# Eight gate chunks by Strassen's scheme, all gates by way of DRAM, a written order for the branches, and the residual made during the attention

## The chip, the cores and the metric

The kernel runs on one core of a Trainium2 chip. Its time is the device time in microseconds of one launch, given as the median of several runs. The engines are TensorE (PE: matmuls; PEld: its weight loads), VectorE (DVE), ScalarE (ACT), GpSimd (POOL) and SyncE (SP, which here only issues DMAs). Each engine works through its own queue in program order and waits at the head of the queue for what other engines or DMAs have still to deliver.

## The reference

One encoder block on 1024 tokens of width 1024. The stage that matters here lies between the attention and the feed-forward part:

```python
proj = h @ w_in[l] + b_in[l]
qa, ka, va, qb, kb, vb, ga, gb = jnp.split(proj, IN_SPLITS, axis=-1)
...
y_na = neighbourhood_attention(qa, ka, va, na_rpb[l]) @ w_branch_na[l]
y_swa = windowed_gqa_with_sink(qb, kb, vb, swa_sink[l]) @ w_branch_swa[l]
mixed = jax.nn.sigmoid(ga) * y_na + jax.nn.sigmoid(gb) * y_swa
attn_out = mixed @ w_out[l] + b_out[l]
h = layer_norm(DEEPNORM_ALPHA * h + attn_out, ln1_g[l], ln1_b[l])
```

The two gates `ga` and `gb` are products of the 1024 x 1024 normalised input with 1024 columns of weights each. The residual `DEEPNORM_ALPHA * h + b_out` does not depend on the attention.

## The kernel before

**Three products for one.** Every float32 product is made from high and low parts: `hi*hi + hi*lo + lo*hi` (`gemm3`, lines 219 to 226). An operand is split by a copy on ACT (the high part) and a subtraction on DVE (the low part). A chunk of 128 gate columns takes 2 token halves x 8 pieces of depth x 3 = 48 matmuls of 128x512. `hT` (64 KB of each partition) holds the normalised input, both parts, transposed.

**The attention** (lines 603 to 703) is written out by hand in steps of two query blocks (`steps`, line 668): normalise (`part_a2`), scores (`part_a`), transposes (`part_b`), products with the values (`part_c`). Between them `pump` lets PE do matmuls of the projections, so that it has work while DVE and ACT make the softmax; these "fills" include the gate chunks f = 4 to 7 of both gates (`N_AHEAD = 4`), whose sums go to DRAM (`sg_d`). Sixteen heads of four steps; heads 8 to 15 get 72 fills each, heads 0 to 7 get 48. The fills are used up when the last three steps (62 to 64) come. At each head from 7 on POOL makes the bias of a later head (`na_bias`), from 16 small loads on SP's queue.

**Gates and branches** (lines 704 to 796) are not in a written order: a planner places their instructions, also among the attention's last ones. `oS` holds the attention's output, split (lines 714 to 721). For each f from 0 to 7: for f < 4 two gate chunks are made from `hT` and go through the sigmoid straight from PSUM (lines 770 to 780); for f >= 4 the stored sums are read back from DRAM. Then two branch products per token half (`w_na`, `w_swa`) are multiplied by the gates on DVE and added on POOL into `mx` (lines 785 to 792). In the same stage POOL makes the residual, two operations for each of eight token groups, from DRAM to DRAM (`residual0`, lines 756 to 761), and `wo`, the output projection's weights, is loaded and split (lines 799 to 804).

**Later** the feed-forward products already use the Winograd form of Strassen's scheme; its list of seven products with the PSUM bank of each is

```python
STEPS = ((1, "a"), (2, "b"), (6, "a"), (5, "c"), (7, "a"), (3, "c"), (4, "a"))
```

The functions that the diff touches follow with their line numbers.

Of the kernel before, what the change touches and what calls it, by code (L numbers as in the profile page):

```python
# [75 lines left out]
def encoder_block(ctx, tc, x, w_in, w_na, w_swa, w_out, w_ff1, w_ff2, par, rows, rpbp, sink,  # L76
# [4 lines left out]
    def b32(ap):  # L81
        return ap.bitcast(F32)
# [26 lines left out]
    sg_d = dp.tile([N_AHEAD, 2, 2, P, 512], F32, name="sg_d")  # L109
    e_d = dp.tile([8, 8, 31, 24], F32, name="e_d")  # L110


# [31 lines left out]
    def load_w(srcs):  # L144
        return split_w(dma_w(srcs))
# [7 lines left out]

    hT = r1p.tile([P, 2, NK, S], F32R, tag="r1", name="hT")
    ln = r3p.tile([P, 8, D], F32, tag="r3", name="ln")
    actx = ExitStack()
    ap = actx.enter_context(tc.tile_pool(name="ap", bufs=2, reuse_waits="tile"))

# [236 lines left out]
    def gate_half(i, w, half):  # L395

        f, gi = 8 - N_AHEAD + i // 2, i % 2
        ps = psum("mm")
        yield from gemm3_steps(ps, w, lambda part, k: h_perm(part, k, half))

        def evac():
            s_ = wp.tile([P, 512], F32, tag="wlo2" if i == 1 else "whi2", name="sa", bufs=1)
            ACT.activation(s_, ps, AF.Identity, bias=prm[:, C_G + gi * 8 + f:C_G + gi * 8 + f + 1], scale=1.0)
            nc.sync.dma_start(sg_d[i // 2, gi, half], s_)
        defer(0, evac)

    def gate_ahead(i):
# [132 lines left out]
    def part_c(s):  # L540
# [62 lines left out]
    with tc.manual_schedule(engines=MANUAL):  # L603
# [19 lines left out]
        def pump(n):  # L623
            for _ in range(n):
                if next(fill, "end") == "end":
                    for e in later:
                        e[0] = 0
                    flush()
                    return
                for e in later:  # L630
                    e[0] -= 1
# [33 lines left out]
            pass  # L665
        next(fill)

        def steps(s, n):
# [7 lines left out]
            pump(part[0])  # L676
            if 0 <= s < 64:
# [4 lines left out]
            pump(part[1])  # L682
            if s >= 1:
# [10 lines left out]
        oT = r3p.tile([P, 8, S], F32, tag="r3", name="oT")  # L694
        counts = [CNT[0]] * 8 + [CNT[1]] * 8
        for H in range(16):
            if H >= 7 and H - 7 < 8:
# [3 lines left out]
        for s in range(62, 65):  # L701
            steps(s, TAIL)
        pump(1000)
    actx.close()
    n_w[:] = [0, 3]


    xp = ctx.enter_context(tc.tile_pool(name="xp", bufs=1, side="right", reuse_waits="tile"))
    r2x = ExitStack()
    r2p = r2x.enter_context(tc.tile_pool(name="r2p", bufs=1, side="right", reuse_waits="tile"))  # L710
    oS = r2p.tile([P, 2, 8, S], F32R, tag="r2", name="oS")
    mctx = ExitStack()
    mp = mctx.enter_context(tc.tile_pool(name="mp", bufs=2, reuse_waits="tile"))
    for c in range(8):
        src, hi, lo = oT[:, c, :], oS[:, 0, c, :], oS[:, 1, c, :]
        if c >= 4:

            src = src.rearrange("p (r g c) -> p g r c", g=NCG, c=8)
            hi, lo = (t.rearrange("p (g r c) -> p g r c", g=NCG, c=8) for t in (hi, lo))
        ACT.copy(hi, src)  # L720
        DVE.tensor_tensor(out=lo, in0=src, in1=b32(hi), op=ALU.subtract)
    mx = r3p.tile([P, 8, S], F32, tag="r3", name="mx")

    def o_na(part, k, half):
        return oS[:, part, k, half * 512:(half + 1) * 512]

    def o_swa(part, k, half):
        return oS[:, part, 4 + k, half * 512:(half + 1) * 512]

    def tok(g):  # L730
        return slice(g * P, (g + 1) * P)

    mhl = {}

    def split_mx(g):

        m = xp.tile([P, 2, 8, P], F32R, tag=f"m{g % 2}", name="m")
        mhl[g] = m[:, 0], m[:, 1]
        ACT.copy(m[:, 0], mx[:, :, tok(g)])
        DVE.tensor_tensor(out=m[:, 1], in0=mx[:, :, tok(g)], in1=b32(m[:, 0]), op=ALU.subtract)  # L740

    def branch_w(f):
        fs = slice(f * P, (f + 1) * P)
        return load_w([(0, 4, 0, P, w_na[:, fs]), (4, 4, 0, P, w_swa[:, fs])])


    r01 = xp.tile([P, 2, D], F32, tag="m0", name="r01")
    zr = xp.tile([P, 2, D], F32, tag="m1", name="zr")
    for i in range(2):
        nc.sync.dma_start(r01[:, i, :], row_bc(i))  # L750
    nc.sync.dma_start(zr[:, 0, :], row_bc(2))
    for i in range(2):
        POOL.tensor_scalar(out=r01[:, i, :], in0=r01[:, i, :], scalar1=ALPHA, scalar2=None, op0=ALU.mult)
    POOL.tensor_tensor(out=r01[:, 1, :], in0=r01[:, 1, :], in1=zr[:, 0, :], op=ALU.add)

    def residual0(g):
        z = zr[:, g % 2, :]
        nc.sync.dma_start(z, xn0_d[g])
        POOL.tensor_tensor(out=z, in0=z, in1=r01[:, 0, :], op=ALU.mult)
        POOL.tensor_tensor(out=z, in0=z, in1=r01[:, 1, :], op=ALU.add)  # L760
        nc.sync.dma_start(xr0_d[g], z)

    wbs = {}
    for f in range(8):
        if f < 4:
            residual0(2 * f)
            residual0(2 * f + 1)
        sg = []
        for gi in range(2):
            w = load_w(gate_w(gi, f)) if f < 8 - N_AHEAD else None  # L770
            for half in range(2):
                s_ = mp.tile([P, 512], F32, tag=f"sg{gi}", name="sg")
                sg.append(s_)
                if w is None:
                    nc.sync.dma_start(s_, sg_d[f - 8 + N_AHEAD, gi, half])
                    ACT.activation(s_, s_, AF.Sigmoid)
                    continue
# [3 lines left out]
        for i in (f, f + 1):  # L781
            if i not in wbs and (i == f or 8 - N_AHEAD <= i < 8):
                wbs[i] = branch_w(i)
        wb = wbs[f]
        for half in range(2):
            pa = psum("t")
            gemm3(pa, wb, lambda part, k: o_na(part, k, half), nk=4)
            DVE.tensor_tensor(out=sg[half], in0=pa, in1=sg[half], op=ALU.mult)
            pb = psum("o")
            gemm3(pb, wb, lambda part, k: o_swa(part, k, half), nk=4, k0=4)  # L790
            DVE.tensor_tensor(out=sg[2 + half], in0=pb, in1=sg[2 + half], op=ALU.mult)
            POOL.tensor_tensor(out=mx[:, f, half * 512:(half + 1) * 512], in0=sg[half], in1=sg[2 + half], op=ALU.add)
            if f == 7 and half == 0:
                split_mx(0)
                split_mx(1)
    mctx.close()


    wo = r1p.tile([P, 2, NK, D], F32R, tag="r1", name="wo")
    for k in range(NK):  # L800
        raw = wp.tile([P, D], F32, tag="raw", name="raw", bufs=2)
        nc.sync.dma_start(raw, w_out[k * P:(k + 1) * P, :])
        ACT.copy(wo[:, 0, k, :], raw)
        DVE.tensor_tensor(out=wo[:, 1, k, :], in0=raw, in1=b32(wo[:, 0, k, :]), op=ALU.subtract)
# [143 lines left out]
    with tc.manual_schedule(engines=MANUAL):  # L948
# [28 lines left out]
                raws[2] = head_w(2)  # L977

        def more_ring(i):
            t = xp.tile([P, 2, 2, 512], F32R, tag=f"m{i}", name="twx")  # L980
            ring[0:0] = [t[:, 0], t[:, 1]]

        us, snaps = {}, {}
# [337 lines left out]
        for n, (p, i) in enumerate(seq):  # L1321
# [5 lines left out]
            elif n == 2:  # L1327
                more_tw()
            if n == 12:
                xts.append(xp.tile([P, 2, D], F32, tag="m1", name="rr"))  # L1330
                xts.append(xp.tile([P, 4, 512], F32, tag="m0", name="rst"))
                residual_rows()
            ff1_mm(p, i)
            for f in tails[:2 if p == 1 else 1]:
# [273 lines left out]
```

## Time and profile before

| | us |
|---|---|
| median of 3 runs (1376.11 to 1378.56) | 1377.28 |
| the profiled execution: its time | 1378.37 |
| the profiled execution: its span, first to last instruction | 1376.6 |
| PE busy | 1336.7 |
| DVE busy | 934.1 |
| ACT busy | 679.6 |
| POOL busy | 295.5 |

The granted clock was 0.992 of full on average. A row of the profile is read like this: line of the kernel, engine, operation, output<-inputs, shapes, xcount, then busy time and mean duration, then the idle time of the engine before these instructions and what ended it. In a timeline the first number is the start in us from the first instruction, the second the time that the row's instructions took, and what stands in brackets is idle time before, with who ended it. A table of stages gives for each engine its busy time in the stretch and the number of instructions.

### The profile page before, as it was taken

The page shows a single profiled execution, that of the slowest core. Times are in us where ns is not written, and L with a number is a line of the kernel's source. Part 1 is how long each engine was busy: PE and PEld are TensorE (multiplying, and loading weights), DVE is VectorE, ACT ScalarE, POOL GpSimd, SP SyncE. Part 2 cuts the span into 40 slices and gives each one's busy share as a digit, 9 for nine tenths or more (in the row PEclk, how much of TensorE's full clock was granted, in tenths as well). Part 3 has the DMA queues.
Part 4 walks back from the last instruction along what each step waited for, and adds up shares of the span by engine and source line. Part 5 has one row for each costly group of instructions (what it writes and reads, how often), then busy time and mean ns, then how long its engine had stood idle before and what let it go on. Part 6 is the DMA issues. An engine that isn't in the chain of part 4 may idle for free. (4 is left out here: it accounts for less than half of the span.)

```text
span 1376.6 us, 17188 instructions
## 1 busy us (share of the span) xinstructions
PE 1336.7 (97%) x6312; PEld 1102.1 (80%) x6312; DVE 934.1 (68%) x1553; ACT 679.6 (49%) x1173; POOL 295.5 (21%) x264
## 2 busy tenths in 40 slices
PE   5999999999999999999999999999999999999996
PEld 4788888888888888888888788888887888878884
DVE  7458989877776721244467987676655668787777
ACT  4436666666655611142445755555554533333354
POOL 3332212121120375011000042222100001121218
PEclk9999999999999999999999999999999999999998
DMA  6521021112102444144233576655528554544323
GB/s 217 181 66 43 24 62 44 32 34 51 38 22 77 127 164 156 59 155 151 89 110 130 164 242 205 207 195 181 197 94 319 191 184 145 206 145 179 116 96 123
DMA packets 130165, 179.70 MB, mean 131 GB/s; under 512 B 26400, under 2 KB 82976, under 8 KB 126368
## 3 DMA queue, kind: packets, MB, share of 16 engines
q1 hardware_dynamic: 129648, 178.48, 39.1%
q8 instruction: 49, 0.80, 0.3%
q14 instruction: 36, 0.29, 0.1%
q10 hardware_dynamic: 432, 0.12, 0.0%
HBM read 124.04 MB, written 54.72 MB: 130 GB/s over the span
## 5 line engine op out<-in xcount | busy, mean ns | idle before, releaser
L234 PE MATMUL ps_mm<-hT,whi 128*128 128x512 f32 x832 | 275.8, 406 | 7.2 <-DVE hT L210 2.5
L234 PEld LDWEIGHTS ps_mm<-hT,whi 128*128 128x128 f32 x832 | 154.8, 191 | 38.4 <-DVE kl L298 4.3
L234 PE MATMUL ps_mm<-hT,wlo 128*128 128x512 f32 x416 | 170.7, 410 | 0.0
L494 ACT ACTIVATE ss<-ss,st 128x384 f32<-128x384 f32 (+1 forms) x128 | 74.5, 586 | 64.7 <-DVE st L482 35.0
L1228 ACT CAST t<-stg 128x2048 fp32r<-128x2048 f32 x28 | 53.5, 1909 | 88.6 <-PE ps_o L1360 47.3
L1379 POOL TENSOR_TENSOR acc<-acc,rst 128x512 f32<-128x512 f32 x16 | 30.7, 1917 | 302.4 <-DMA rst<-xr_d 289.5
L1360 PE MATMUL ps_mm<-t,t 128*128 128x512 f32 x384 | 93.0, 397 | 2.3 <-DVE t L1231 1.6
L1360 PE MATMUL ps_s<-t,t 128*128 128x512 f32 x384 | 91.0, 392 | 0.0
L1360 PEld LDWEIGHTS ps_mm<-t,t 128*128 128x128 f32 x384 | 72.9, 191 | 20.0 <-DVE t L1231 2.5
L234 PEld LDWEIGHTS ps_mm<-hT,wlo 128*128 128x128 f32 x416 | 79.3, 191 | 11.5
L1360 PEld LDWEIGHTS ps_s<-t,t 128*128 128x128 f32 x384 | 72.1, 188 | 16.2
L945 PE MATMUL ps_t<-hS,tw 128*128 128x512 f32 x348 | 84.8, 392 | 0.0
L534 ACT CAST pth<-ps_t 128x384 fp32r<-128x384 f32 (+1 forms) x128 | 52.0, 456 | 64.2 <-PE ps_t L531 63.7
L1231 DVE TENSOR_TENSOR t<-stg,t 128x2048 fp32r<-128x2048 f32 x28 | 68.1, 2431 | 14.8 <-ACT t L1228 14.8
L945 PEld LDWEIGHTS ps_t<-hS,tw 128*128 128x128 f32 x348 | 65.4, 188 | 14.8
L150 DVE TENSOR_TENSOR wlo<-raw,whi 128x1024 fp32r<-128x1024 f32 x16 | 24.9, 1558 | 76.1 <-ACT whi L149 76.0
L1360 PE MATMUL ps_t<-t,t 128*128 128x512 f32 x288 | 68.6, 392 | 0.3 <-DVE t L1231 0.3
L1360 PE MATMUL ps_o<-t,t 128*128 128x512 f32 x288 | 68.0, 392 | 0.0
L537 DVE TENSOR_TENSOR ptl<-ps_t,pth 128x384 fp32r<-128x384 f32 (+1 forms) x128 | 61.2, 518 | 7.2 <-ACT pth L534 6.8
L1360 PEld LDWEIGHTS ps_t<-t,t 128*128 128x128 f32 x288 | 54.0, 188 | 13.0 <-DVE t L1231 1.2
L1360 PEld LDWEIGHTS ps_o<-t,t 128*128 128x128 f32 x288 | 54.1, 188 | 11.9
L1112 DVE TENSOR_TENSOR usl<-usl 128x512 f32<-128x512 f32 x64 | 50.8, 794 | 14.8 <-ACT usl L1005 11.1
(258 smaller groups left out, 3139.6 us busy)
## 6 DMA issues: line engine op xcount, KB each, us to landing
us_d<-usl SPq DMA_DIRECT2D x112, 256.0 KB
stg<-us_d SPq DMA_DIRECT2D x28, 1024.0 KB
raw<-in_w_ff SPq DMA_DIRECT2D x36, 512.0 KB
raw<-in_w_in SPq DMA_DIRECT2D x26, 512.0 KB
w2b<-in_w_ff SPq DMA_DIRECT2D x7, 1024.0 KB
w2a<-in_w_ff SPq DMA_DIRECT2D x5, 1024.0 KB
sg_d<-sa SPq DMA_DIRECT2D x16, 256.0 KB
xn_d<-ln SPq DMA_DIRECT2D x8, 512.0 KB
```

The lines of the kernel that those rows point to most:

```text
L150: DVE.tensor_tensor(out=lo, in0=raw, in1=b32(hi), op=ALU.subtract)
L234: PE.matmul(ps, a[:, k, :], act(b, k), start=(k == 0 and i == 0), stop=(k == NK - 1 and i == 2))
L494: ACT.activation(p[:, :n], p[:, :n], AF.Exp, bias=st[:, 2 + i:3 + i], scale=0.125, accum_out=st[:, 4 + i:5 + i])
L534: ACT.copy(pth[:, a:b, :], pv)
L537: DVE.tensor_tensor(out=ptl[:, a:b, :], in0=pv, in1=b32(pth[:, a:b, :]), op=ALU.subtract)
L945: PE.matmul(ps, ww, act[:, part, k, :], start=(first and k == 0 and m == 0), stop=(k == 3 and m == 2), skip_group_check=True)
L1112: DVE.tensor_tensor(out=out, in0=a, in1=b, op=op)
L1228: ACT.copy(slot[:, :, 0, :], src)
L1231: DVE.tensor_tensor(out=slot[:, :, 1, :], in0=src, in1=b32(slot[:, :, 0, :]), op=ALU.subtract)
L1360: PE.matmul(ps, st[:, a, part, j * P:(j + 1) * P], w[:, a, wpart, :], start=(first and a == 0 and m == 0), stop=(a == 3 and m == 2), skip_ ...
L1379: POOL.tensor_tensor(out=z, in0=z, in1=t, op=ALU.add)
```

## The change

**The last eight gate chunks** (f = 0 to 3 of both gates) become four pairs p of 256 columns: p = 0 and 1 are chunks 0/1 and 2/3 of the first gate, p = 2 and 3 those of the second. With the input cut in depth (K1, K2) and tokens (T1, T2), A11 = hT[K1,T1], A12 = hT[K2,T1], A21 = hT[K1,T2], A22 = hT[K2,T2], and the weights of a pair cut in depth and columns (B11 to B22), seven products of 12 matmuls each (a block (p, i)) replace eight:

- i = 1: A11 B11, i = 2: A12 B21; C11 is their sum
- i = 6: S2 (B22 - (B12 - B11)), i = 5: S1 (B12 - B11), i = 7: S3 (B22 - B12), i = 3: S4 B22, i = 4: A22 (B21 - the sum of i = 6)
- S1 = A21 + A22, S2 = S1 - A11, S3 = A22 - S2, S4 = A12 - S2

PSUM bank a gathers products 1, 6, 7 and 4 in turn and is read out after each; the other banks are added on DVE. All finished gates go to DRAM (`sg_d` grows from 4 to 8 chunks), and the branches read every gate back and apply the sigmoid then.

**The order** of everything from the end of the attention to the last split of `wo` is written out for all engines. S1 is summed in the last head (`s1_sum`, one DVE operation of 128x2048 after each of three steps). The weights of blocks (0,1), (0,2), (1,1) and (1,2) are loaded and split in the last steps; blocks (0,1) and (0,2) run inside steps 63 and 64, the others after the attention. The last evacuation of the attention (`last_evac`) is put off behind the first sum for S2. `graw` holds a pair's raw columns: pairs 2 and 0 share one 8 KB buffer (`x0p`), pair 1 takes the one in which S1 was summed (`x1p`), pair 3 half of `gt`, whose other half holds S2's sum. S1, S2, S4 and `gt` lie in the 64 KB where `oS` is put afterwards, in four pieces.

**The residual** moves into the attention: its rows into head 6, one token group per head into heads 7 to 14 (load after the head's first step, the two POOL operations after the second, the store after the fourth).

```diff
+x1p = ctx.enter_context(tc.tile_pool(name="x1p", bufs=1, side="right", reuse_waits="tile"))
...
-            ACT.copy(oo, po[64:P, :])
-            DVE.tensor_tensor(out=oo, in0=po[0:64, :], in1=oo, op=ALU.add)
+            def evac():
+                ACT.copy(oo, po[64:P, :])
+                DVE.tensor_tensor(out=oo, in0=po[0:64, :], in1=oo, op=ALU.add)
+            if s == 63:
+                last_evac.append(evac)
+            else:
+                evac()
...
+        def residual0(g, i):
+            if i == 0:
+                zs0[g] = zp.tile([P, D], F32, tag="z", name="zr")
+                nc.sync.dma_start(zs0[g], xn0_d[g])
+            elif i == 1:
+                for r, op in ((0, ALU.mult), (1, ALU.add)):
+                    POOL.tensor_tensor(out=zs0[g], in0=zs0[g], in1=r01[:, r, :], op=op)
+            elif i == 3:
+                nc.sync.dma_start(xr0_d[g], zs0[g])
...
+        def g_sums(p, i):
+            if i == 6:
+                gT2[p] = gp.tile([P, 4, P], F32, tag="ts", name="gT2")
+                sub(gB(p, 1, 1), gB(p, 1, 2), gB(p, 1, 1))
+                sub(gT2[p], gB(p, 2, 2), gB(p, 1, 1))
+            elif i == 7:
+                sub(gB(p, 1, 2), gB(p, 2, 2), gB(p, 1, 2))
+            elif i == 4:
+                sub(gB(p, 2, 1), gB(p, 2, 1), gT2[p])
+        def g_hi(p, i, src=None):
+            gtags.append(gtags.pop(0))
+            t = gw[p, i] = wp.tile([P, 2, 4, P], F32R, tag=gtags[-1], name="gw", bufs=1)
+            ACT.copy(t[:, 0], g_src(p, i) if src is None else src)
+        def g_lo(p, i, src=None):
+            t = gw[p, i]
+            DVE.tensor_tensor(out=t[:, 1], in0=g_src(p, i) if src is None else src, in1=b32(t[:, 0]), op=ALU.subtract)
+        def g_mm(p, i):
+            ...
+            for k in range(4):
+                for m, (a, b) in enumerate(((0, 0), (0, 1), (1, 0))):
+                    PE.matmul(ps, w[:, a, k, :], act[:, b, k, :], start=(first and k == 0 and m == 0),
+                              stop=(k == 3 and m == 2), skip_group_check=True)
...
+        steps(62, TAIL)
+        steps(63, TAIL, lambda: g_mm(0, 1))
+        head_prep(1, 1)
+        steps(64, TAIL, None, lambda: g_mm(0, 2))
...
+        f_add(g2, g1, part("A11", 0), ALU.subtract)
+        last_evac[0]()
+        g_hi(2, 1)
+        form_hi("S1", g1)
+        g_lo(2, 1)
+        g_after(0, 1)
...
+        g_do(1, 1)
+        g_sums(2, 6)
+        form_lo("S2", g2)
...
+        form_hi("S3", g2)
+        g_sums(2, 7)
+        g_sums(3, 7)
+        g_hi(2, 7)
+        form_lo("S3", g2)
+        g_lo(2, 7)
...
+        g_sums(2, 4)
+        g_hi(2, 4)
+        g_do(2, 3)
+        g_after(2, 3)
+        g_lo(2, 4)
+        g_load(0)
+        g_fetch(0, 0)
+        g_fetch(0, 1)
+        g_load(1)
+        g_fetch(1, 0)
+        g_fetch(1, 1)
...
+        g_do(2, 4)
+        g_sums(0, 6)
+        g_hi(0, 6)
+        o_hi(1)
+        g_sums(1, 6)
+        g_lo(0, 6)
...
-            w = load_w(gate_w(gi, f)) if f < 8 - N_AHEAD else None
...
-                ps = psum(pstags[gi])
-                gemm3(ps, w, lambda part, k: h_perm(part, k, half))
-                ACT.activation(s_, ps, AF.Sigmoid, bias=prm[:, C_G + gi * 8 + f:C_G + gi * 8 + f + 1], scale=1.0)
...
+        def sg_load():
+            f, gi, half = k = sgs.pop(0)
+            s_ = sg[k] = mp.tile([P, 512], F32, tag="sg", name="sg")
+            nc.sync.dma_start(s_, sg_d[f, gi, half])
...
+                branch(f, half)
+                if sgs:
+                    sg_load()
+                    sg_load()
```

More of the change, by code (lines that the diff above doesn't have):

```diff
@@ L666, in encoder_block, with steps @@
         next(fill)
-        def steps(s, n):
+        last_evac = []
+        def steps(s, n, before_b=None, before_c=None):
             part = [int(n * SPLIT[0]), int(n * SPLIT[1])]
@@ L714, in encoder_block @@
[L714 to L744, printed above, removed]
@@ L747, in encoder_block @@
[L747 to L761, printed above, removed]
@@ L796, in encoder_block @@
[L796 to L804, printed above, removed]
+                if 7 <= H < 15:
+                    residual0(H - 7, i)
+                if H == 15:
+                    if i == 2:
+                        head_w0(0)
+                    if i == 0:
+                        g1 = x1p.tile([P, 4, 512], F32, tag="m", name="g1")
+                    else:
+                        s1_sum(i - 1)
@@ new lines, in encoder_block, with f_add, part, form_hi @@
+        gctx = ExitStack()
+        gp = gctx.enter_context(tc.tile_pool(name="gp", bufs=2, reuse_waits="tile"))
+        for i, n in enumerate(("S1", "S2", "S4")):
+            gop[n] = r2p.tile([P, 2, 4, 512], F32R, tag=f"r2{i}", name="g" + n)
+        gt = r2p.tile([P, 2, 8, 256], F32, tag="r23", name="gt")
+        def f_add(out, a, b, op=ALU.add):
+            DVE.tensor_tensor(out=out, in0=a, in1=b, op=op)
+        def part(n, i):
+            return b32(gop[n][:, i])
+        def form_hi(n, src):
+            ACT.copy(gop[n][:, 0], src)
@@ new lines, in o_hi, with o_lo, g_do @@
+        def o_hi(c):
+            src, hi, lo = o_views(c)
+            ACT.copy(hi, src)
+        def o_lo(c):
+            src, hi, lo = o_views(c)
+            DVE.tensor_tensor(out=lo, in0=src, in1=b32(hi), op=ALU.subtract)
+        def g_do(p, i):
+            g_mm(p, i)
+            if i in (1, 6, 5, 4):
+                g_after(p, i)
+        g_load(2)
+        g_load(3)
+        for c in range(2):
+            g_fetch(2, c)
+            g_fetch(3, c)
+        f_add(g2, g1, part("A11", 0), ALU.subtract)
@@ new lines, in encoder_block, with b_load, b_split @@
+        g_load(1)
+        g_fetch(1, 0)
+        g_fetch(1, 1)
+        g_sums(3, 4)
+        g_hi(3, 4)
+        g_do(3, 3)
+        g_after(3, 3)
+        g_lo(3, 4)
+        g_do(2, 7)
+        g_after(2, 7)
+        g_do(3, 7)
+        g_after(3, 7)
+        def b_load(f):
+            fs = slice(f * P, (f + 1) * P)
+            braw[f] = dma_w([(0, 4, 0, P, w_na[:, fs]), (4, 4, 0, P, w_swa[:, fs])])
+        def b_split(f):
+            i = (2, x, 1 - x)[f % 3]
+            w = bws[f] = [wp.tile([P, 8, P], F32R, tag=f"{t}{i}", name=t, bufs=1) for t in ("whi", "wlo")]
+            ACT.copy(w[0], braw[f])
+            DVE.tensor_tensor(out=w[1], in0=braw[f], in1=b32(w[0]), op=ALU.subtract)
@@ new lines, in sigmoid, with wo_load, wo_split @@
+        def sigmoid(f, gi, half):
+            s_ = sg[f, gi, half]
+            if f < 8 - N_AHEAD:
+                ACT.activation(s_, s_, AF.Sigmoid, bias=prm[:, C_G + gi * 8 + f:C_G + gi * 8 + f + 1], scale=1.0)
+            else:
+                ACT.activation(s_, s_, AF.Sigmoid)
+        def wo_load(k):
+            raw = wo_raw[k] = wp.tile([P, D], F32, tag="raw", name="raw", bufs=2)
+            nc.sync.dma_start(raw, w_out[k * P:(k + 1) * P, :])
+        def wo_split(k):
+            ACT.copy(wo[:, 0, k, :], wo_raw[k])
+            DVE.tensor_tensor(out=wo[:, 1, k, :], in0=wo_raw[k], in1=b32(wo[:, 0, k, :]), op=ALU.subtract)
@@ new lines, in branch @@
+        def branch(f, half):
+            both = []
+            for gi, (act, tag) in enumerate(((o_na, "t"), (o_swa, "o"))):
+                ps = psum(tag)
+                gemm3(ps, bws[f], lambda part, k: act(part, k, half), nk=4, k0=4 * gi)
+                s_ = sg[f, gi, half]
+                both.append(s_)
+                DVE.tensor_tensor(out=s_, in0=ps, in1=s_, op=ALU.mult)
+            POOL.tensor_tensor(out=mx[:, f, half * 512:(half + 1) * 512], in0=both[0], in1=both[1], op=ALU.add)
```

260 lines of the change are left out of this document (217 added, 43 removed).

## The prediction

> **What bounds the kernel now.** I read the page's busy shares first, then a table of stages (busy time of each engine in each stretch), then the groups of instructions and the timeline of the stage between the attention and the output projection, which is the stage the change rewrites.
>
> ```profile
> PE 1336.7 (97%) x6312; PEld 1102.1 (80%) x6312; DVE 934.1 (68%) x1553; ACT 679.6 (49%) x1173; POOL 295.5 (21%) x264
> ```
>
> ```profile
> 205.00:265.00 60.00, 57.67 (x338) 49.68 (x337) 52.78 (x145) 43.45 (x107) 13.17 (x19) 1.00 0.16 37
> 325.00:385.00 60.00, 59.79 (x342) 51.72 (x341) 45.00 (x120) 37.60 (x85) 12.60 (x23) 1.00 0.18 41
> ...
> 465.00:640.90 175.90, 175.90 (x768) 143.54 (x767) 63.81 (x62) 52.99 (x65) 70.41 (x34) 1.00 0.46 144
> ```
>
> The columns are PE, PEld, DVE, ACT, POOL, granted clock, DMA share and GB/s. TensorE is the bound. In the gate and branch stage (465 to 640.9) it has no idle time at all, at full clock, while DVE works 36% and ACT 30% of it. In the attention PE loses 2.3 us per 60 where DVE is 88% busy and 0.2 where DVE is 75% busy. So in this stage only fewer matmuls shorten the kernel, and any wait that the new order creates is paid in full.
>
> ```profile
> 463.76 0.89 DVE L537 TENSOR_TENSOR ptl<-ps_t,pth 128x384 fp32r<-128x384 f32 x2
> ...
> 464.93 0.27 PE L566 MATMUL ps_o<-pth,vv 128*128 128x128 f32 x1
> 465.04 0.45 PE L225 MATMUL ps_mm<-hT,whi 128*128 128x512 f32 x1
> 465.33 0.40 PE L226 MATMUL ps_mm<-hT,wlo 128*128 128x512 f32 x1
> 465.56 0.39 PE L224 MATMUL ps_mm<-hT,whi 128*128 128x512 f32 x1
> 465.79 0.40 PE L225 MATMUL ps_mm<-hT,whi 128*128 128x512 f32 x1
> ```
>
> A gate matmul comes every 0.2267 us (465.33, 465.56, 465.79); its 0.39 us is pipelined.
>
> **Removed: 48 matmuls.** The last eight gate chunks are 8 x 48 = 384 matmuls. Strassen's scheme does two chunks (a pair p of 256 columns) in 7 blocks of 12, so 4 x 84 = 336. 48 x 0.2267 = 10.9 us come off PE. A second gain is the one gap in the attention's last steps, which a block now covers:
>
> ```profile
> 462.60 0.55 PE L531 MATMUL ps_t<-ident,ss 128*128 128x128 f32 x3 [0.47 <-DVE ptl L537]
> ```
>
> That is 0.5 us. Together: minus 11.4.
>
> **Added: DVE work at the stage's front.** The prices are rows of the feed-forward's start, where the same kinds of operation run back to back (chain of waits: start, time, what):
>
> ```profile
> 759.24 2.20 DVE hS L1146
> 761.44 0.60 DVE tw L1105
> 762.04 0.61 DVE twx L1105
> ```
>
> A 128x2048 subtraction takes 2.20 us of DVE, a 128x512 one 0.60. Let T0 be the moment PE ends the attention's last matmul and starts block (1,1); a block (p,i) takes 12 x 0.2267 = 2.72. Block (2,7) is the thirteenth, due at T0 + 32.6. Before it DVE must do, in the written order, ten wide operations (g2 twice, the low parts of S2 and S1, g1 twice, g2, the low part of S4, g2, the low part of S3) and 22 narrow ones (the deferred evacuation, weight sums, low parts, evacuations): 10 x 2.20 + 22 x 0.60 = 35.2. It can begin about 1.7 before T0, while PE does block (0,2) and the last four products of the attention; sooner brings nothing, since the second operation, the evacuation, needs T0. So it ends at 33.5, plus 0.6 for a wait on ACT's copy of S3 and for hand-overs: PE waits **1.5 us**. From below 0. From above 3.2, if the memory of the first sum is still held by attention tiles until T0, so that DVE begins there; the trace of before cannot show which. I take the early start, because DVE's last attention subtraction (463.76) ends before PE's last product (464.93).
>
> **Added: four loads in the middle.** The columns of pairs 0 and 1 are fetched only once DVE is done with pair 2's buffer (low part of block (2,4)), four narrow operations after (2,7)'s: T0 + 36.5. The first block that needs them, (0,6), also stands behind the weight sums of (1,6) on DVE, so all four 512 KB loads must land. The nearest rows are such loads in a row at the feed-forward's start:
>
> ```profile
> 744.18 0.38 SPq L924 DMA_DIRECT2D raw<-in_w_ff x1
> 744.66 3.35 SPq L1068 DMA_DIRECT2D raw<-in_w_ff x4
> ```
>
> ```profile
> 747.51 8.66 DMA raw<-in_w_ff
> ```
>
> Five loads, issued from 744.18, have landed at 747.51 + 8.66 = 756.17: 2.4 us each. A faster row is 1 MB of 512-byte runs:
>
> ```profile
> 425.60:429.90 4.30, 4.30 (x25) 3.69 (x24) 3.02 (x10) 1.89 (x5) 0.00 (x0) 1.00 0.89 245
> 504.80:506.60 1.80, 1.80 (x10) 1.49 (x9) 0.00 (x0) 0.00 (x0) 1.80 (x1) 1.00 0.99 295
> ```
>
> Four loads by the first row take 9.6 and land at 46.1; two sums and a low part make 48.0 with hand-overs 48.5. PE wants (0,6) after 16 blocks and the wait above, at 43.5 + 1.5 = 45.0. It waits **3.5 us**. At 295 GB/s (2.1 MB in 7.1, and 1.3 from issue to the first packet) the wait is 1.8; with each load a quarter slower, behind the stores of finished gates, 5.7. I take 3.5, by the row with several loads queued.
>
> **Added: the clock.** Such a gap has a price of its own:
>
> ```profile
> 1047.70:1051.10 3.40, 1.67 (x7) 0.74 (x5) 1.81 (x1) 3.37 (x4) 0.00 (x0) 1.00 1.03 390
> 1051.10:1054.50 3.40, 2.87 (x7) 2.29 (x8) 3.38 (x3) 3.29 (x5) 0.00 (x0) 0.50 1.07 389
> ```
>
> A stretch of 3.4 us in which PE worked 1.67 was followed by one at half clock. Wherever the stretches fall, a gap of 3.5 puts at least 1.75 us of idleness into one of them. A stretch at half clock costs 3.4 / 2 = **1.7 us**; nothing if the gap stays under about 1.5, two stretches (3.4) if it is over 5. The Trainium skill ("TensorE: Matmul & The Clock Gate", "HAM oscillation") says that idle gaps over some 3.4 us are what brings the clock down; by that rule a gap of 3.5 would seldom hold a whole idle window and the sum would be 1.7 lower. The rows of this case show half an idle window to be enough, so I go by them.
>
> **After that, nothing.** From (0,6) on PE has ten blocks, 27.2 us, and DVE some 21 (twelve low parts and sums, four evacuations, seven 1024-wide low parts of the attention's output and weights). In the branches 24 matmuls per half last 5.5 us against two products, a sigmoid pair and a split on each engine. The gates read back from DRAM add 16 stores and 16 loads of 256 KB at a DMA share of 0.46; they are read two halves (11 us) ahead. The former planner's order had no PE gap here, so writing it out gains nothing.
>
> **Moved: the residual.** 16 POOL operations of 2.6 us, three on the rows, eight loads and eight stores go from the gates into heads 6 to 14 of the attention.
>
> ```profile
> L759 POOL TENSOR_TENSOR zr<-zr,r 128x1024 f32<-128x1024 f32 x8 | 21.0, 2625 | 13.6 <-DMA zr<-xn_d 13.6
> L150 DVE TENSOR_TENSOR wlo<-raw,whi 128x1024 fp32r<-128x1024 f32 x14 | 22.5, 1605 | 72.5 <-ACT whi L149 72.4
> L804 DVE TENSOR_TENSOR wo<-raw,wo 128x1024 fp32r<-128x1024 f32 x8 | 9.8, 1225 | 12.6 <-ACT wo L803 12.6
> ```
>
> ```profile
> L510 DVE TENSOR_SCALAR ss<-ss,st x128: 346/416/1456, 101.9 to 457.4; 128x384 f32<-128x384 f32 x96, 128x256 f32<-128x256 f32 x32
> ```
>
> Beside these POOL operations a DVE subtraction took 1.61 us on average, without them 1.23: 0.38 x 14 = 5.3 us over 19 POOL operations. In the attention DVE would lose the same 5 to 8 us over nine heads, about 2 us per 60. Where DVE is 75% busy that is covered by its 15 idle us; heads 6 and 7, at 88%, pass some on. I put **0.7 us** (0 to 3). If the cover is gone it is the slow rival below. The Trainium skill ("SBUF — State Buffer", "SBUF: two separate sides") has the port that both share as an exclusive lock for a whole instruction; by it each of the 19 could hold DVE for its full length, and L510's longest, 1.46 against 0.42, agrees for single cases, while the mean above says that most pass; what that lock would cost here in full is worked out from rows as rival 3. On SP's queue the stores wait for POOL, as they do now:
>
> ```profile
> SPq L761 <- POOL zr L760: 45.0, 8, 8.7
> SPq L141 <- DVE wlo L429: 92.7, 11, 19.4
> ```
>
> Weight loads queue behind them, but the second row shows those loads themselves waiting up to 19 us for a free buffer, a block ahead of need: no cost. The three sums of S1 in the last head add 6.6 us to DVE in 18 in which it idles a quarter, 4.6: it enters the last steps up to 2 us late, but there block (0,1) gives PE 2.72 us of other work: no cost (2 without that cover).
>
> **Sum.** -10.9 - 0.5 + 1.5 + 3.5 + 1.7 + 0.7 = -4.0. The profiled execution took 1378.37 us with a span of 1376.6; the span becomes 1372.6, the execution 1374.4. The median of the runs is 1377.28, 1.1 below the profiled one, so I predict 1377.3 - 4.0 = **1373.3**.
>
> **Rivals.** (1) The loads are hidden, because DVE reaches (2,4) sooner or the queue runs at the fast row's rate: waits of 0.5 and 1.0, no clock step: -11.4 + 1.5 + 0.7 = -9.2, **1368.1**. For it: the fast row of 295 GB/s. Against: the written DVE order, which puts both pairs' sums before the first low part. (2) The memory of the new tiles is held until T0, and the first four loads start only then: 3.2 at the front, 5.7 in the middle, two stretches at half clock 3.4: -11.4 + 12.3 + 0.7 = +1.6, **1378.9**. For it: the new tiles lie where the attention's were. Against: queries and keys are last read several steps earlier. (3) The slower side: POOL locks DVE out in the attention for whole operations. Heads of 24 us then carry two of 2.2 us each (the longest excess of L150 in this trace:
>
> ```profile
> 477.74 3.41 DVE L150 TENSOR_TENSOR wlo<-raw,whi 128x1024 fp32r<-128x1024 f32 x1
> ```
>
> 3.41 against 1.23), that is 10.8 per 60: DVE goes from 45.0 to 55.8 of 60, beyond the 52.8 at which PE lost 2.3. At 3.5 lost per 60 over the 190 us of heads 7 to 14: 11 us, -4.0 - 0.7 + 11 = +6.3, **1383.6**. It decides from 4 us on, that is from about 0.25 us of PE wait per moved operation. (4) PE's pitch for the summed operands is not the gates' one: the branches, whose operands lie where the sums will, run at 0.2333:
>
> ```profile
> 633.17 0.39 PE L224 MATMUL ps_o<-oS,whi 128*128 128x512 f32 x1
> ...
> 633.87 0.40 PE L224 MATMUL ps_o<-oS,whi 128*128 128x512 f32 x1
> ```
>
> Three matmuls in 0.70 us. The 144 matmuls on S1, S2 and S4 would cost 144 x 0.0066 = 1.0 more, **1374.3**; I give it no chance of its own, it lies inside the forecast's range.
>
> **Chances.** The forecast 0.45 (own range 1370 to 1376.5; a fifth of it has no clock step, 1371.6), (1) 0.22, (2) 0.20, (3) 0.08; 0.05 for a gain that is lost some other way, near 1377. A measurement of this kernel can tell about 0.2%, 2.75 us: faster is under 1374.5, slower over 1380.0. Faster: 0.33 of the forecast, 0.22 of (1), 0.02 of (2): 0.57. Slower: (3) and 0.05 of (2): 0.13. Same: 0.30. The range 1366.5 to 1379.0 leaves out (3) and the far ends of (1) and (2).
>
> **What would show it.** 336 gate matmuls and 0.2267 us between them; one PE gap of 2 to 5 us before the sixth block group, ended by DVE after a load of the gate columns, with a half-clock stretch behind it; a smaller one before (2,7), ended by DVE; no new PE gap in 225 to 445. Wrong if the gap is missing (rival 1), if PE waits already before (2,1) (rival 2), or if PE's idle time in heads 7 to 14 grows over 3 us (rival 3).

## The result, and the profile after

The changed kernel takes 1396.08 us (median of 4 runs, 1395.19 to 1398.36) against 1377.1 for the kernel before on the same chip: a ratio of 1.0139, 95% interval 1.0122 to 1.0157. It is 19 us slower; 1373.3 was forecast, with 1379.0 as the upper end. The profiled execution took 1395.19 us with a span of 1393.4, 16.8 longer than the span before. Two of the seven executions of run 1 below, at 1463 and 3397 us, stood far from the rest and are left out of its median.

The page's busy share of TensorE, after:

```profile
PE 1340.0 (96%) x6264; PEld 1101.3 (79%) x6264; DVE 1000.6 (72%) x1614; ACT 703.4 (50%) x1213; POOL 307.5 (22%) x264
```

48 matmuls fewer (6312 to 6264), yet PE is busy 3 us longer: part of its work ran at half clock. The table of stages after (columns as in the prediction) says where:

```profile
205.00:265.00 60.00, 54.62 (x310) 46.57 (x309) 55.40 (x134) 39.77 (x97) 28.24 (x25) 0.97 0.21 60
265.00:325.00 60.00, 56.78 (x312) 48.01 (x311) 48.70 (x112) 33.05 (x76) 22.24 (x22) 0.97 0.27 78
325.00:385.00 60.00, 55.15 (x293) 46.64 (x291) 44.30 (x104) 35.02 (x78) 19.01 (x20) 0.94 0.26 71
385.00:445.00 60.00, 56.43 (x299) 47.98 (x300) 47.46 (x114) 33.13 (x78) 19.00 (x20) 0.94 0.15 48
...
491.74:659.20 167.46, 163.94 (x699) 131.53 (x698) 103.07 (x118) 77.98 (x104) 31.23 (x15) 0.99 0.47 147
```

The first four rows are the attention's heads with the moved residual. PE idles 17.0 of their 240 us; before it was 4.1 (the rows 205 and 325 of the prediction and those at 265 and 385). The clock, 1.00 before, is 0.94 to 0.97: six stretches of 3.4 us at half speed, 10.2 us of work. 12.9 of idleness and 10.2 of clock make 23.1.

The landmarks agree. The attention's last product starts at 491.74, before at 464.93: 26.8 later. Its last steps now hold two gate blocks (24 x 0.2267 = 5.4), and before they held 4 gate matmuls (0.9), so the attention itself is 22.3 longer. From there to the first product of the output projection it is 167.5 now (491.74 to 659.2) and 175.9 before; with those two blocks and 4 matmuls counted in, 172.9 against 176.8, a gain of 3.9. The rest of the kernel is 1.5 shorter. 22.3 - 3.9 - 1.5 = 16.9, the span's difference. The gates did nearly what was forecast; the loss is in the attention, where 0.7 us was put.

PE's two longest waits on DVE, after, then before (line waited for: us in all, times, longest):

```profile
PE ps_mm L237 <- DVE kl L301: 9.9, 5, 2.8
PE ps_s L476 <- DVE st L479: 6.6, 5, 2.2
```

```profile
PE ps_s L473 <- DVE st L476: 2.3, 3, 1.1
PE ps_mm L234 <- DVE kl L298: 2.3, 5, 1.1
```

They are the same two as before, four and three times as much. The timeline of the changed kernel shows one such place, first POOL, then DVE, then PE:

```profile
263.19 5.06 POOL L736 TENSOR_TENSOR zr<-zr,r 128x1024 f32<-128x1024 f32 x2
```

```profile
263.57 2.25 DVE L509 TENSOR_TENSOR st<-st 128x2 f32<-128x2 f32 x1
...
266.05 2.68 DVE L513 TENSOR_SCALAR ss<-ss,st 128x384 f32<-128x384 f32 x2
```

```profile
269.25 0.44 PE L476 MATMUL ps_s<-kh,q 128*128 128x384 f32 x1 [1.99 <-DVE st L479]
```

While POOL runs its two residual operations (263.19 to 268.25), a DVE addition of 128x2 numbers, elsewhere 0.16 us in the median, takes 2.25; the two scalings, elsewhere 0.75, take 2.68. Each ends just behind one of the two POOL operations. PE's next scores go to a PSUM buffer that DVE has yet to read (L479, behind the scalings), and PE waits 1.99. What follows is in the table of stages, cut finely:

```profile
267.50:270.90 3.40, 1.65 (x8) 1.34 (x9) 3.24 (x9) 0.98 (x3) 0.75 (x1) 0.99 0.45 167
270.90:274.30 3.40, 3.40 (x12) 2.81 (x11) 0.58 (x1) 3.33 (x7) 0.00 (x0) 0.50 0.20 38
```

A stretch in which PE worked 1.65 of 3.40, then one at half clock.

The larger sum, 9.9 us behind L301, comes about by a longer way. At the next such place (POOL's two operations from 316.78 to 321.70) the rows are, for DVE, ACT and PE:

```profile
319.65 2.53 DVE L513 TENSOR_SCALAR ss<-ss,st 128x384 f32<-128x384 f32 x2
...
327.17 0.68 DVE L576 TENSOR_TENSOR oT<-ps_o,oT 64x512 f32<-64x512 f32 x1 [2.92 <-ACT oT L575]
```

```profile
323.36 0.51 ACT L497 ACTIVATE ss<-ss,st 128x256 f32<-128x256 f32 x1 [4.08 <-DVE st L483]
```

```profile
329.44 1.22 PE L237 MATMUL ps_mm<-hT,whi 128*128 128x512 f32 x2 [2.78 <-DVE kl L301]
```

POOL holds a cast (L303) and the scalings, together 3.0 us more than in run 1 below. So the scores are read late, and ACT waits 4.08 for them, 1.08 in run 1. The rest of the chain is as in run 1, only 3 us later: ACT's exponentials and three evacuations, its copy (L575) for which DVE waits 2.92, and L301, which empties the PSUM buffer for PE's next projection. PE waits 2.78, until 329.44, nearly 8 us after POOL's last operation ended.

### The profile page after: what moved, and what is told of

It reads as the page before. It is cut to its first block, busy times and chain, and to the rows that moved or that the text cites. A ratio compares the mean times of both kernels' runs of the same rounds, so it can differ in the third digit from the quotient of the medians.

```text
span 1393.4 us, 17267 instructions
## 1 busy us (share of the span) xinstructions
PE 1340.0 (96%) x6264; PEld 1101.3 (79%) x6264; DVE 1000.6 (72%) x1614; ACT 703.4 (50%) x1213; POOL 307.5 (22%) x264
## 4 chain that ended last, share of the span: by engine, by line
PE 71%; DVE 16%; ACT 6%; POOL 2%; issue 2%; DMA 2%; SPq 0%; POOLq 0%; DVEq 0%; ACTq 0%
PE ps_mm L237 12%; PE ps_mm L1681 6%; PE ps_o L1266 6%; PE ps_mm L1266 5%; PE ps_t L1266 5%; PE ps_s L1681 5%; PE ps_t L1681 5%; PE ps_o L1681 4%; DVE ss L513 2%; PE ps_s L1266 2%; DVE ss L479 2%; ACT ss L497 2%; PE ps_o L569 1%; PE ps_mm L809 1%; POOL acc L1767 1%
## 5 line engine op out<-in xcount | busy, mean ns | idle before, releaser
L237 PE MATMUL ps_mm<-hT,whi 128*128 128x512 f32 x832 | 280.5, 412 | 14.4 <-DVE kl L301 9.9
L237 PEld LDWEIGHTS ps_mm<-hT,whi 128*128 128x128 f32 x832 | 157.9, 194 | 46.9 <-DVE kl L301 11.8
L237 PE MATMUL ps_mm<-hT,wlo 128*128 128x512 f32 x416 | 173.2, 416 | 0.0
L237 PEld LDWEIGHTS ps_mm<-hT,wlo 128*128 128x128 f32 x416 | 80.8, 194 | 11.7
L1095 POOL TENSOR_TENSOR mx<-sg 128x512 f32<-128x512 f32 x16 | 33.4, 2090 | 196.2 <-DVE sg L1094 196.2
L513 DVE TENSOR_SCALAR ss<-ss,st 128x384 f32<-128x384 f32 (+1 forms) x128 | 67.9, 572 | 2.2
```

What stands on the lines that cost most here:

```text
L237: PE.matmul(ps, a[:, k, :], act(b, k), start=(k == 0 and i == 0), stop=(k == NK - 1 and i == 2))
L513: DVE.tensor_scalar(out=p[:, :n], in0=p[:, :n], scalar1=st[:, 6 + i:7 + i], scalar2=None, op0=ALU.mult)
```

## The experiments

Theory A: POOL's residual operations hold DVE off, in the attention, and PE starves. Its two forms: the *length* of one POOL instruction decides (A1), or the *amount* of POOL work (A2). Rivals: the moved transfers (B); the rebuilt gates and branches, wherever the residual stands (C). The kernel before ran beside each group of runs, at 1377.3 to 1377.8 us.

**1. Without the POOL operations.** The eight loads and stores stay; the residual's scaling and shift are left out.

```diff
-                for r, op in ((0, ALU.mult), (1, ALU.add)):
-                    POOL.tensor_tensor(out=zs0[g], in0=zs0[g], in1=r01[:, r, :], op=op)
+                pass
```

> The changed kernel with the 16 POOL operations of the residual left out of the attention; its loads and stores stay, and the three POOL operations on the rows too. It leaves out the residual's scale and shift, so its output is not the reference's. Theory A (POOL's operations hold DVE up, DVE is late with the projections' evacuation, PE waits and its clock is halved): 1396.1 falls by about 20 to 1375 to 1378, PE idle time in 205 to 445 us falls from 17.0 to about 4, and the half-clock stretches there vanish but for those of head 6. Theory B (the moved loads and stores on SP's queue delay weight loads or the bias tables): stays within 3 us of 1396.

1373.70 us, ratio 0.9972 (0.9959 to 0.9985). One row of its table of stages:

```profile
325.00:385.00 60.00, 59.80 (x342) 51.68 (x341) 45.20 (x121) 37.47 (x85) 12.59 (x23) 1.00 0.30 85
```

PE idles 0.2 of 60 again, at full clock, with the transfers in place. The 16 POOL operations cost 22 us; the transfers are not the cause.

**2. The same work in short pieces.** Each of the 16 operations becomes eight.

```diff
-                    POOL.tensor_tensor(out=zs0[g], in0=zs0[g], in1=r01[:, r, :], op=op)
+                    for c in range(8):
+                        cs = slice(c * P, (c + 1) * P)
+                        POOL.tensor_tensor(out=zs0[g][:, cs], in0=zs0[g][:, cs], in1=r01[:, r, cs], op=op)
```

> The changed kernel with each of the 16 POOL operations cut into 8 of 128 columns, the same work in shorter instructions. Theory A1 (what costs is that one POOL instruction holds the shared port for its whole 2.4 us, two in a row 4.9): DVE gets in between, longest DVE scale (2.42 us now) falls under 1 us, time 1376 to 1382. Theory A2 (what costs is the amount of POOL work, a shared bandwidth): within 3 us of 1396.

1374.97 us, ratio 0.9985 (0.9976 to 0.9995). The sum over the four stretches, then the place of above on POOL and on DVE:

```profile
sum 240.00, PE 233.22 PEld 200.57 DVE 192.67 ACT 151.94 POOL 109.32; mean PE 58.31 PEld 50.14 DVE 48.17 ACT 37.98 POOL 27.33
```

```profile
261.61 7.14 POOL L738 TENSOR_TENSOR zr<-zr,r 128x128 f32<-128x128 f32 x16
```

```profile
261.98 0.31 DVE L509 TENSOR_TENSOR st<-st 128x2 f32<-128x2 f32 x1
...
262.52 0.89 DVE L513 TENSOR_SCALAR ss<-ss,st 128x384 f32<-128x384 f32 x2
```

POOL is busy *longer* (109.3 against 88.5) and its group lasts 7.14 for 5.06, but DVE's addition takes 0.31 and the scalings 0.89. A1 stands, A2 falls.

**3. Pieces of half a row**, and **4. one whole-row operation per step** in place of both at once:

```diff
+                    for c in range(2):
+                        cs = slice(c * 512, (c + 1) * 512)
```

> The changed kernel with each of the residual's 16 GpSimd operations cut into two of 512 columns (about 1.25 us each), in the same place and order. If VectorE gets in between two GpSimd instructions, the longest delay is near 1.3 us, under what TensorE has in stock before a weight split is late: 1376 to 1382 us, few or no stretches at half clock between 205 and 445 us. If GpSimd's instructions follow each other without letting VectorE in, as with whole rows: 1390 us or more.

```diff
             elif i == 1:
-                for r, op in ((0, ALU.mult), (1, ALU.add)):
-                    POOL.tensor_tensor(out=zs0[g], in0=zs0[g], in1=r01[:, r, :], op=op)
+                POOL.tensor_tensor(out=zs0[g], in0=zs0[g], in1=r01[:, 0, :], op=ALU.mult)
+            elif i == 2:
+                POOL.tensor_tensor(out=zs0[g], in0=zs0[g], in1=r01[:, 1, :], op=ALU.add)
```

> The changed kernel with the residual's two GpSimd operations of a group in two steps (multiplication in the second, addition in the third) in place of both in one: single holds of about 2.4 us, not two in a row (4.9 us). Theory 'one instruction's hold delays VectorE, and two in a row delay it past what TensorE has in stock': shorter waits, fewer of them followed by the half clock, 1380 to 1390 us. Rival 'each hold of 2.4 us is enough by itself, their number counts': 1395 us, as the changed kernel. Rival 'only the doubling matters': 1375 us, as with pieces of 128 columns.

Halves: 1388.60 us (ratio 1.0078, 1.0064 to 1.0091). One per step: 1396.18 (1.0138, 1.0125 to 1.0152). The first lies between the two figures given for it. The second is the rival's figure, but the edit did not do what it was written for. POOL has nothing else in its queue between the two steps, and still runs the two operations one right behind the other:

```profile
262.95 2.59 POOL L735 TENSOR_TENSOR zr<-zr,r 128x1024 f32<-128x1024 f32 x1
265.62 2.36 POOL L737 TENSOR_TENSOR zr<-zr,r 128x1024 f32<-128x1024 f32 x1
```

So run 4 only repeats the changed kernel. What a single hold of 2.4 us would cost stays open.

The place of above with halves, POOL then DVE:

```profile
262.81 5.37 POOL L738 TENSOR_TENSOR zr<-zr,r 128x512 f32<-128x512 f32 x4
```

```profile
263.16 1.14 DVE L509 TENSOR_TENSOR st<-st 128x2 f32<-128x2 f32 x1
...
264.54 2.51 DVE L513 TENSOR_SCALAR ss<-ss,st 128x384 f32<-128x384 f32 x2
```

The addition's time over the three sizes is 2.25, 1.14 and 0.31 for POOL instructions of 2.42, 1.34 and 0.50 us on average: at this place it waits out the instruction under way, and no more. Halves don't remove the loss, because each further DVE operation that meets POOL waits again: the two scalings cost 1.76 more than the usual 0.75, nearly as with whole rows.

**5. The move alone**, in the kernel before, with whole rows; and **6. with pieces of 128 columns**. The edit is the residual's part of the change and nothing else of it.

> The kernel before with one part of the change alone: the residual made in the attention's heads 6 to 14, gates and branches as they were. Theory A or B: 1377 + 20 to 22 = 1397 to 1400, with half-clock stretches in heads 7 to 14. Theory C: within 3 us of 1377.

1401.01 us, ratio 1.0175 (1.016 to 1.019). Its longest wait in the attention is the one of above: PE at L237 behind L301, 11.3 us in five waits, the longest 2.8.

> The kernel before with its residual moved into the attention, as in the run of the move alone, but in pieces of 128 columns. This is the price of the move as I had forecast it: 0.7 us (0 to 3) on 1377.3, so 1377 to 1380 us. If the pieces only helped together with Strassen's gates, it stays near the 1401 us of the move with whole rows.

1380.64 us, ratio 1.0024 (1.0015 to 1.0033). So the move costs 23.7 us as it is written and 2.8 (2.1 to 4.5) in pieces. The gates' part of the change is the difference to the whole: 1396.1 - 1401.0 = -4.9 with whole rows, 1375.0 - 1380.6 = -5.7 with pieces (-4.7 and -5.2, each run taken against the kernel before that ran beside it).

**7. The residual back among the branches**, whole rows; and **8. there in pieces**:

```diff
-                if 7 <= H < 15:
-                    residual0(H - 7, i)
...
                 if sgs:
                     sg_load()
                     sg_load()
+                residual_at(2 * f + half)
```

> The changed kernel with the residual's loads, POOL operations and stores made in the branches instead of the attention; all else stays. Theory A or B (the move is what costs): 1370 to 1375, below the kernel before by the 4 us of the gates. Theory C (Strassen's gates or the written order cost it): 1390 or more, and the stage from the attention's last product to the output projection is longer than before.

> The kernel with the residual put back into the branches (1397.0 us with whole rows), its GpSimd operations in pieces of 128 columns. If the loss there was again the length of one GpSimd instruction, it goes as in the attention: 1373 to 1376 us. If it was my order (GpSimd's sums for the branches queued behind the residual, whose total is then even longer, about 8 us a group for 5.8), the waits for the branches' weights stay: 1390 us or more.

1396.97 us (ratio 1.0145, 1.0129 to 1.0161) and 1410.5 (1.0242, 1.0225 to 1.0259). The 1370 to 1375 of theory A was missed, and by its time alone run 7 would speak for C; but runs 1, 5 and 6 leave the gates a gain of about 5 us. The attention is as before in both runs, and PE now waits in the branches; the waits with whole rows and with pieces:

```profile
PE ps_t L227 <- ACT whi L995: 9.8, 3, 3.3
PE ps_t L229 <- DVE wlo L996: 3.0, 3, 1.3
```

```profile
PE ps_t L227 <- ACT whi L995: 10.9, 3, 4.6
PE ps_t L227 <- DVE sg L1090: 5.3, 1, 5.3
PE ps_t L229 <- DVE wlo L996: 5.2, 3, 4.2
```

POOL's timeline there, with pieces:

```profile
573.72 6.71 POOL L1111 TENSOR_TENSOR zr<-zr,r 128x128 f32<-128x128 f32 x16 [5.59 <-DMA zr<-xn_d]
580.39 1.29 POOL L1091 TENSOR_TENSOR mx<-sg 128x512 f32<-128x512 f32 x1
581.64 6.71 POOL L1111 TENSOR_TENSOR zr<-zr,r 128x128 f32<-128x128 f32 x16
588.30 1.27 POOL L1091 TENSOR_TENSOR mx<-sg 128x512 f32<-128x512 f32 x1
```

And SP's queue in the same run, at the read-back of the gates (L1066):

```profile
SPq L1066 <- POOL mx L1091: 74.6, 9, 12.7
```

By these rows the order of POOL's queue is the first cause. The branches' sums (`mx`) come between two groups, so the tiles of the read-back gates (`sg`) come free late and SP loads them late. ACT has the split of the branches' next weights behind the sigmoids of these gates; the first wait, ACT's rows:

```profile
569.67 1.44 ACT L1071 ACTIVATE sg<-sg,prm 128x512 f32<-128x512 f32 x2 [7.54 <-DMA sg<-sg_d]
571.02 1.03 ACT L995 CAST whi<-raw 128x1024 fp32r<-128x1024 f32 x1
```

With pieces a group lasts longer, and holds of another length are added. DVE, then PE:

```profile
578.68 11.97 DVE L1081 TENSOR_TENSOR wo<-raw,wo 128x1024 fp32r<-128x1024 f32 x1 [4.18 <-ACT wo L1080]
```

```profile
591.40 0.77 PE L227 MATMUL ps_t<-oS,whi 128*128 128x512 f32 x1 [5.27 <-DVE sg L1090]
```

This subtraction, 1.23 elsewhere, began during a piece and ended 1.08 behind the sum of 588.30: POOL ran 22 more instructions without a pause, and DVE got in between none of them. A second one, at 637.27, took 4.90 in the same way, and PE's wait of 4.2 behind L996 hangs on it; run 10 has both again (11.93 and 4.91). So an instruction's length is not always the limit of a hold. This place of mine is no proof that none among the branches would do; no other order was run there, and the kernel before had its residual in the gate chunks ahead of them.

**9. A version that beats both: pieces, and two lines of the gates' order.** The prediction put the wait before block (0,6) down to the second pair's sums, written ahead of the first pair's low part. **10** is the same two lines with run 8's residual.

```diff
         g_hi(0, 6)
         o_hi(1)
+        g_lo(0, 6)
+        o_lo(1)
         g_sums(1, 6)
-        g_lo(0, 6)
         g_hi(1, 6)
-        o_lo(1)
```

> Pieces of 128 columns as before, and in Strassen's block the two lows of the sixth product's first pair and of the branch weights are made ahead of the second pair's sums, not behind them (one line moved). If the wait before block (0,6) comes from the four loads that the second pair's sums need, its 2.7 us and the stretch at half clock behind it (1.7 to 1.9 us) go: 1370 to 1371 us against 1375.0 with pieces alone. If the first pair's own two loads are the late ones, most of the wait stays, or moves to block (1,6): 1373 to 1375 us.

> The same with the two lows ahead of the second pair's sums in Strassen's block. Takes away the wait before block (0,6): 2 to 4 us under the run with pieces alone in the same place; if those weights are split late in the branches all the same, nothing is gained on 1390 us or more.

Run 9 takes 1372.81 us, ratio 0.9967 (0.9955 to 0.998): 5.0 us under the kernel before that ran beside it (4.5 by the ratio) and 23 under the change. Run 10 takes 1407.29, 3.2 under run 8, as expected. PE at block (0,6), with pieces alone and then in run 9:

```profile
521.29 6.92 PE L811 MATMUL ps_mm<-gS,gw 128*128 128x512 f32 x22 [2.71 <-DVE gw L801]
528.05 11.32 PE L811 MATMUL ps_t<-gS,gw 128*128 128x512 f32 x48
539.21 11.06 PE L811 MATMUL ps_mm<-hT,gw 128*128 128x512 f32 x48
```

```profile
517.91 3.32 PE L811 MATMUL ps_mm<-gS,gw 128*128 128x512 f32 x12
522.09 3.31 PE L811 MATMUL ps_mm<-gS,gw 128*128 128x512 f32 x12 [0.86 <-ACT gw L797]
```

The wait falls from 2.71 to 0.86 and moves to the next block, (1,6), whose columns are loaded last, and the half clock behind it is gone: the next row starts 2.8 us sooner (525.24). Of that, 2.2 us arrive in the medians, short of the 4 to 5 I expected; one difference between the two profiled executions is a half-clock stretch in the feed-forward part (from 1047.6 us), which run 9 has and the run with pieces alone has not.

## Why the prediction was wrong

**The failed step: "Moved: the residual", 0.7 us (0 to 3).** Measured: 23.7 us alone in the kernel before, 22.3 in the changed kernel's trace. The sum of the other steps holds, so the whole miss is this one term. Three things in it were wrong.

*The mean was read as a chance to pass.* I divided the excess of 14 DVE subtractions by 14 and by POOL's 19 operations and concluded "that most pass". The rows behind that mean, in the trace of before, DVE then POOL:

```profile
487.03 2.30 DVE L150 TENSOR_TENSOR wlo<-raw,whi 128x1024 fp32r<-128x1024 f32 x1 [5.88 <-ACT whi L149]
498.55 1.47 DVE L150 TENSOR_TENSOR wlo<-raw,whi 128x1024 fp32r<-128x1024 f32 x1 [0.42 <-ACT whi L149]
```

```profile
477.44 2.63 POOL L754 TENSOR_TENSOR r<-r,zr 128x1024 f32<-128x1024 f32 x1
...
485.84 2.41 POOL L759 TENSOR_TENSOR zr<-zr,r 128x1024 f32<-128x1024 f32 x1
...
496.53 2.40 POOL L759 TENSOR_TENSOR zr<-zr,r 128x1024 f32<-128x1024 f32 x1 [4.94 <-DMA zr<-xn_d]
```

The subtractions at 477.74 (3.41, quoted in the prediction), 487.03 and 498.55 began while POOL was running; they ended at 481.15, 489.33 and 500.02, that is 1.08, 1.08 and 1.09 us after the POOL operation's end, nearly their whole duration of 1.23. Three more, at 564.15, 597.67 and 609.29, began during a branch sum (L792) and ended 1.08 behind it. So six of the 14 began while POOL was running, and all six waited it out; the other eight, the one at 510.04 for example, took the plain 1.23. And 1.8 of the 5.3 us came from the branch sums, not from the operations that were to move. The Trainium skill ("SBUF — State Buffer", "SBUF: two separate sides") says that whichever starts first has the shared ports for its whole instruction; I set it aside for the mean, and the trace that I had agreed with it.

*The excess on DVE.* 5 to 8 us were forecast. Run 1 has the same DVE operations without POOL's: taken one by one, those of the attention add up to 20.5 us more in the changed kernel, 1.3 per POOL operation.

*The cover.* I set DVE's idle share of the stage, 15 us in 60, against it. But it counts which operation is held. Five of the eight pairs of POOL operations met the addition or the cast and then the scalings, 3.0 to 4.1 us together, and PE waited 2.0 to 2.8: it had 0.2 to 2.1 us of other work. The three pairs at 291, 347 and 402 met little more than one weight subtraction (L432), and PE did not wait. DVE's idle time elsewhere covers none of a hold on that chain: 20.5 us of DVE became 12.9 us of PE idleness, and the clock nearly doubled that. The prediction priced a half-clock step for the gates (1.7) and didn't ask for it here.

**Rival 3** named this mechanism, its place and its sign, with a chance of 0.08, at 1383.6. Its 11 us counted PE's idleness (12.9 measured) without the clock (10.2 more). That the 11 came near is luck: it was worked out from a DVE busy 55.8 us of 60, and in three of the four stretches DVE was busy 44.3 to 48.7 while PE lost 3.2 to 4.9.

**The gates, term by term.** *-10.9:* the count and the pitch are as forecast on `hT`; on the sums the pitch is that of rival 4: 48 matmuls take 11.32 on `gS` and 11.06 on `hT` (rows above), 0.8 us over the 144. *Wait before (2,7), 1.5:* measured 0.52. *Wait before (0,6), 3.5, and half clock, 1.7:* the changed kernel's timeline, PE, then DVE:

```profile
525.95 11.70 PE L809 MATMUL ps_o<-hT,gw 128*128 128x512 f32 x47 [0.52 <-DVE hT L850]
...
541.03 1.22 PE L809 MATMUL ps_mm<-gS,gw 128*128 128x512 f32 x2 [2.81 <-DVE gw L799]
```

```profile
538.96 0.69 DVE L779 TENSOR_TENSOR graw<-graw 128x512 f32<-128x512 f32 x1 [2.17 <-DMA graw<-in_w_in]
```

Block (1,1) starts at 491.85, T0 of the prediction. The loads go at 529.17, T0 + 37.3 (36.5 forecast), the last lands at T0 + 47.1 (46.1) and PE goes on at T0 + 49.2 (48.5) after 2.81 us. From there 22 matmuls take 6.53 us to the start of the next row (547.56), for 5.1 at the pitch on `gS`: 1.4 of clock. With these terms the stage should be -10.9 + 0.8 + 0.5 + 2.8 + 1.4 = -5.4; by the landmarks it is -3.9. Most of the difference lies beside the waits: from start to start the matmuls at 525.03 to 526.89, 531.44 to 532.23 and 537.50 to 544.08 lose 1.2, 0.3 and 4.5 us against their pitch, 6.0 and not 4.7. That makes -4.1. The rest's 1.5 is not traced. Forecast were -4.7 with the attention's 0.5; the runs give -4.9 and -5.7. The bounds of the wait before (0,6) were added up wrongly: by the terms given the fast row makes 2.3, not 1.8, and the slow one 5.9, not 5.7; the forecast's 3.5 is not touched. Rivals 1 and 2 are out: the loads are not hidden, and PE doesn't wait before (2,1).

**The sum with the one term corrected:** -10.9 - 0.5 + 1.5 + 3.5 + 1.7 + 23.7 = +19.0, and 19.0 was measured. To the tenth that is luck: the two waits and the clock step were put 2.0 too high, and the pitch (0.8) and what lies beside the waits (1.3) were put at nothing. The same sum with the 2.8 of the pieces gives -1.9; run 2 measured -2.3.

## What to carry to other kernels

Before work is moved between VectorE and GpSimd, or beside one of them, look at single rows, not at a group's mean: take the instructions that began while the other engine ran, and see whether they end where its instruction ends. If they do, the price is set by how long the other engine runs without letting go and by what hangs on the delayed instruction, not by busy shares. Short pieces (here 128 columns, 0.5 us) kept nearly all of the overlap in the attention; among the branches a whole row of them held one DVE operation for 12 us, so the rows are to be read again after such a change. And a move that puts waits of some 2 us on TensorE's path is to be priced with the half clock that can follow each.

## What the runs showed of the hardware

Which DVE operations wait for POOL depends on their operands. Another place in the changed kernel's timeline, POOL then DVE:

```profile
316.78 4.92 POOL L736 TENSOR_TENSOR zr<-zr,r 128x1024 f32<-128x1024 f32 x2
```

```profile
317.06 0.76 DVE L301 SCALAR_TENSOR_TENSOR kl<-ps_mm,prm,kh 64x512 fp32r<-64x512 f32 x1
317.86 1.59 DVE L303 CAST kl<-kl 64x512 fp32r<-64x512 f32 x1
```

L301, which reads PSUM, takes the same 0.76 as without POOL; the cast behind it, from SBUF to SBUF, takes 1.59 where 0.42 is usual. In the rows of the result the 128x2 addition and the scaling, all in SBUF, are held, while a 128x2 RECIPROCAL at 319.45 takes its usual 0.17 in the middle of the POOL row above. The Trainium skill's section ("SBUF — State Buffer", "SBUF: two separate sides") names DVE operations with two SBUF inputs or in a two-port mode, and these rows agree with it, though none shows the mode in which an operation ran. The engine that starts second waits, whichever it is: in the trace of before the subtraction at 527.71 takes its plain 1.23, and POOL's operation begun at 527.96 takes 3.25 for 2.4. Whether DVE gets in between POOL instructions that follow each other without a pause differs: a subtraction of 128x1024 beside the pieces took 1.59 in run 2 (at 289.61) and 11.97 in run 8, and no run shows what decides it. POOL's price for pieces is moderate: 16 of 128 columns take 7.14 us, 4 of 512 take 5.37, 2 of 1024 take 5.06.

In the changed kernel the half clock came after waits of 2.0 to 2.8 us, well under the 3.4 that the Trainium skill gives ("TensorE: Matmul & The Clock Gate", "HAM oscillation"); the measurement decides. Not each such wait brought it: in run 3 three waits of 2.1, 2.1 and 2.8 us did not. The half-clock stretches begin on a grid of 3.41 us. In the changed kernel, run 3 and run 5 each stretch of this grid between 205 and 560 us in which PE worked 0.6 to 1.65 us was followed by half clock; where it worked 1.71 or more, as around those three waits, none was, except that twice the half clock lasted a second stretch. So it is the share of such a stretch that counts here, about half, and where a wait falls in it.
